# Input projection of a hybrid block in five passes instead of three, with TensorE's order tied to the recurrences

## The chip, the cores and the metric

The kernel runs on one NeuronCore of one Trainium2 chip. The metric is device time in microseconds (us). Three runs of the kernel before took 3179.27, 3181.92 and 3189.05 us; the median, 3181.92, is its time. Engines: PE (TensorE: matrix products; PEld are its weight loads), DVE (VectorE), ACT (ScalarE), POOL (GpSimd), SP (SyncE, which issues nearly all DMAs). Each takes its instructions strictly in the order in which they stand in the program.

## What is computed

One layer over 2048 tokens and 16 learned ones in front, all in float32. An input projection feeds three head groups: RG-LRU, forgetting attention and RWKV-7. Cut to what matters here:

```python
p = rms_norm(h, norm_mix_pre) @ w_in          # 1024 -> 512 (a) + 1544 (b) + 1024 (c) columns
oa = rg_lru_group(xa, ya, ...)                # from a: a scan over the tokens
ob = forgetting_attention_group(q, k, v, f)   # from b: softmax with the cumulative log of forget gates f
oc = rwkv7_group(pc, ...)                     # from c: S = S*w - (S kk)(kk a) + v k, out = S r, token by token
h = h + rms_norm(concat(oa, ob, oc) @ w_out, norm_mix_post)
f = causal_dwconv(rms_norm(h, norm_ffn_pre) @ ffn_up)
h = h + rms_norm((gelu(gate) * val) @ ffn_down, norm_ffn_post)
```

## The kernel before

Products that need float32 are split into rounded halves and done as three products (`mm3`, L150 to L152). Stages follow each other: input projection, attention, output projection (W_out), feed-forward up and down.

**Input projection.** The tokens are cut into three parts (784, 768 and 512), each of two blocks. For a part, `w_in_norm` loads its tiles of 128 tokens (7, 6 and 4), normalises and transposes them (tile `pst`, L121) and splits them into `xh` and `xl`, of which there is one set: a part's operands can be written only when the part before has been read. `w_in_part` then works through the weight columns in units of 128: first the forget gate (`psf`, L248), then twelve units for the recurrences (eight c, four a), then twelve for the attention (four each of k, v, q). A unit loads 512 KB of weights, splits them (ACT L144, DVE L145), makes 24 products for each of the two blocks (tile `psp`), evacuates them and stores them to DRAM: c and a to `scr_p`, the attention's to others. v is transposed first (`psv`). `core.evac` (L55, L57) takes ACT and DVE by turns.

**Recurrences.** They read `scr_p` in nine blocks of 256 tokens (the last has 64). `lru_block` is the RG-LRU. `Rwkv.block` prepares a block of RWKV: products for decay and rate (L869, L875), the norm of the keys (gat, L883), a reciprocal root on DVE (L73 to L77), its spreading (L902), the bonus (L922), then `chunks`: score matrices (L946), transposes (L975), a triangular solve on POOL and DVE (L989, L990) by way of DRAM, and, after the solve of the next block, the block's ending (L1013 to L1168: inverses, states, output, group norm). These products have the tiles `eps` (one PSUM bank) and `rps` (two banks). Both are written as generators; a `yield` ends a piece, some 13 to a block.

**What sets the order.** `Beside` holds the pieces. After part 0's gate and twelve units (`READY = 13`) they are added; from then on each unit is followed by `PACE = 1.5` pieces. After each third unit one step of `up_sums` (L1440 to L1449) loads 1 MB of feed-forward weights, forms four sums on POOL and stores them. What is left of the pieces is written out behind the last unit, the attention behind that. A scheduler then places the instructions of each engine by when it expects them ready, and the written order decides where several are; so an engine's order need not be the written one. `tc.issue_after(x)` tells it to place what is inside behind instruction x; it adds no wait between engines.

Of the kernel before, what the change touches and what calls it, by code (L numbers as in the profile page):

```python
# [12 lines left out]
AF = mybir.ActivationFunctionType  # L13
ALU = mybir.AluOpType
# [4 lines left out]
P = 128  # L19
# [166 lines left out]
def w_in_step(core, pools, psum, weights, block, kind, c0, scr):  # L186

    nc = core.nc
    wh, wl = weights
    st = pools["st"]  # L190
    t0, n, tl, hi, lo = block
    ps = psum.tile([P, 512], F32, tag="mm", name=core.n("psp"))
    for k in range(KD):
        mm3(nc, ps[:, :n], wh[:, k], wl[:, k], hi[:, k], lo[:, k], k == 0, k == KD - 1)
    if kind in ("q", "k"):
        sc = 0.125 if kind == "q" else 1.0
        r0 = c0 - (512 if kind == "q" else 1024)
        oh = st.tile([P, 400], F32R, tag="sth", name=core.n("sth"))
        ol = st.tile([P, 400], F32R, tag="stl", name=core.n("stl"), bufs=1)
        nc.scalar.activation(oh[:, :n], ps[:, :n], AF.Copy, scale=sc)  # L200
        nc.vector.scalar_tensor_tensor(ol[:, :n], ps[:, :n], sc, oh[:, :n], op0=ALU.mult, op1=ALU.subtract)
        nc.sync.dma_start(scr[kind + "h"][r0 : r0 + P, t0 : t0 + n], oh[:, :n].bitcast(F32))
        nc.sync.dma_start(scr[kind + "l"][r0 : r0 + P, t0 : t0 + n], ol[:, :n].bitcast(F32))
        return
    o = st.tile([P, 400], F32, tag="sth", name=core.n("stp"))
    core.evac(o[:, :n], ps[:, :n])
    if kind != "v":
        r0 = c0 if kind == "a" else c0 - 2056 + A_ROWS
        nc.sync.dma_start(scr["p"][r0 : r0 + P, PAD + t0 : PAD + t0 + n], o[:, :n])
        return  # L210

    def turn():

        r0 = c0 - 1536
        pt = psum.tile([P, 4, P], F32, tag="mm", name=core.n("psv"))
        for i, (s, rows) in enumerate(tl):
            nc.tensor.transpose(pt[:rows, i], o[:, s - t0 : s - t0 + rows], core.ident[:])
        ot = st.tile([P, 4, P], F32, tag="stv", name=core.n("stv"), bufs=1)
        i0 = 0
        if tl[0][1] < P:  # L220
            s, rows = tl[0]
            core.evac(ot[:rows, 0], pt[:rows, 0])
            nc.sync.dma_start(scr["v"][s : s + rows, r0 : r0 + P], ot[:rows, 0])
            i0 = 1
        m = len(tl)
        core.evac(ot[:, i0:m], pt[:, i0:m])
        s = tl[i0][0]
        nc.sync.dma_start(
            scr["v"][s : s + P * (m - i0), r0 : r0 + P].rearrange("(j p) c -> p j c", p=P), ot[:, i0:m]
        )  # L230

    return turn
# [22 lines left out]
    yield  # L255


def w_in_part(core, pools, psum, w_in, blocks, scr):
    yield from w_in_gate(core, pools, psum, w_in, blocks, scr)
    units = [("c", 2056 + P * i) for i in range(8)] + [("a", P * i) for i in range(4)]  # L260
    units += [(s, c + P * i) for s, c in (("k", 1024), ("v", 1536), ("q", 512)) for i in range(4)]
    waiting = [None]

    def step(*args):

        after = w_in_step(core, pools, psum, *args, scr)
        if waiting[0]:
            waiting[0]()
        waiting[0] = after

    for kind, c0 in units[:-2]:
        w = w_in_weights(core, pools, w_in, c0)
        for block in blocks:
            step(w, block, kind, c0)
        yield

    last = [(w_in_weights(core, pools, w_in, c0), kind, c0) for kind, c0 in units[-2:]]
    for block in blocks:
        for w, kind, c0 in last:
            step(w, block, kind, c0)  # L280
        yield
# [109 lines left out]
class Attn:  # L391
# [248 lines left out]
    AHEAD = 2  # L640
# [66 lines left out]
CH = 64  # L707
# [91 lines left out]
class Rwkv:  # L799
# [127 lines left out]
    def chunks(self, b, nch, sg, rav, bk, wc, bon):  # L927
# [38 lines left out]
        for q in range(parts):  # L966
            nc.sync.dma_start(ia[q * nblk : (q + 1) * nblk, :], da[:ni].rearrange("i q s t -> (i q) (s t)"))
        bkv = bk[:].rearrange("p c a t -> p c (a t)")
        tt(bkv, bkv, wc[:].to_broadcast([P, m2, 2 * CH]), op=ALU.mult)
        for c in range(0, m2, 4):  # L970
            m = min(4, m2 - c)
            for src, dst in ((bk, sc), (rav[:, :, 1:3], w3)):
# [85 lines left out]
        for i0 in range(0, ni, 4):  # L1058
# [5 lines left out]
            nc.scalar.activation(w3[0:64, i0 : i0 + m, 0:64], ps[0:64, :m, 64:128], AF.Copy)  # L1064
        yield
        gt, rp = self.t([P, m2, CH], "gt"), rav[:, :, 0]
        tt(
            gt[:], k["id2"][:].rearrange("p (o t) -> p o t", o=1).to_broadcast([P, m2, CH]),
            wc[:].to_broadcast([P, m2, CH]), op=ALU.mult,
        )  # L1070
# [150 lines left out]
def lru_block(core, R, scr, k, b):  # L1221
# [50 lines left out]

    ya = R.raw(256, c0, c0 + n)
    nc.scalar.activation(y, ya, AF.Square)
    nc.vector.tensor_scalar(y, y, 0.044715, 1.0, op0=ALU.mult, op1=ALU.add)
    tt(y, y, ya, op=ALU.mult)
    nc.scalar.activation(y, y, AF.Tanh, scale=0.7978845608028654)
    stt(y, y, 1.0, ya, op0=ALU.add, op1=ALU.mult)
    stt(u, u, 0.5, y, op0=ALU.mult, op1=ALU.mult)
# [410 lines left out]

READY = 13
PACE = 1.5

WIDE = (0, 5)

# [5 lines left out]
class Beside:  # L1703
# [14 lines left out]
                self.gens.pop(0)  # L1718
        return False

    def advance(self):
        self.due += self.pace if self.gens else 0.0
        while self.due >= 1.0:
            self.due -= 1.0
            if not self.step():
                break
# [31 lines left out]
def hybrid_block_kernel(ctx: ExitStack, tc: tile.TileContext, args, out):  # L1758
# [8 lines left out]
    def run(gen):  # L1767
        for _ in gen:
            pass
# [14 lines left out]
    with ExitStack() as p1:  # L1784
        core.const = pool(p1, "const1", 1)
        dp = pool(p1, "dp", 2, space=DRAM)
        rec = ExitStack()
        ps_rw = pool(rec, "ps_rw", 2, space=PSUM, **right)
        ps_ae = pool(rec, "ps_ae", 1, space=PSUM, **right)
        gp = pool(rec, "gp", 1, **right)  # L1790
        rp = pool(rec, "rp", 1, **right)
        with ExitStack() as p1a:
            ps_mm = pool(p1a, "ps_mm", 5, space=PSUM)
            g_pre = spread(pool(p1a, "gpre", 1), a["norm_mix_pre"], "g_pre")
            pools = {"xn": pool(p1a, "xn", 1), "nt": pool(p1a, "nt", 4), "w": pool(p1a, "w", 2), "st": pool(p1a, "st", 2)}
            sums = up_sums(core, pool(p1a, "us", 1), a["ffn_up"], scr)
            following = w_in_norm(core, pools, ps_mm, x, meta, g_pre, 0)
            for part in range(3):
                blocks = following
                if part == 0:  # L1800
                    zeros = pools["st"].tile([P, PAD], F32, tag="sth", name="zeros")
                    nc.vector.memset(zeros[:], 0.0)
                    for r in range(0, A_ROWS + C_ROWS, P):
                        nc.gpsimd.dma_start(scr["p"][r : r + P, 0:PAD], zeros[:])
                units = w_in_part(core, pools, ps_mm, a["w_in"], blocks, scr)
                for _ in range(READY if part == 0 else 0):
                    next(units)
                if part == 0:
                    attn_consts(core)
                    rk = rwkv_consts(  # L1810
                        core, gp, ps_ae,
                        {
                            s[5:]: (v.rearrange("h d -> (h d)") if s == "rwkv_r_k" else v)
                            for s, v in a.items() if s.startswith("rwkv_")
                        },
                    )
                    lk = lru_consts(
                        core, gp, ps_ae,
                        {
                            "conv_w": a["lru_conv_w"], "conv_b": a["lru_conv_b"], "ga_w": a["lru_gate_a_w"],  # L1820
                            "ga_b": a["lru_gate_a_b"], "gx_w": a["lru_gate_x_w"], "gx_b": a["lru_gate_x_b"],
                            "lam": a["lru_lambda"],
                        },
                    )
                    columns(core, gp, ps_ae, [a["ffn_conv"].rearrange("i (r p) -> (i r) p", p=P)], "", cw)
                    R = Rwkv(core, rp, dp, ps_rw, ps_ae, scr, rk)
                    beside = Beside(PACE)
                for i, _ in enumerate(units, READY + 1 if part == 0 else 1):
                    if i == READY + 1:
                        beside.add(recurrences(core, R, lk, a["fox_f_bias"], scr, blocks, part))  # L1830
                    beside.advance()
                    if i % 3 == 0:
                        next(sums, None)
                run(sums) if part == 2 else None
                if part < 2:
                    following = w_in_norm(core, pools, ps_mm, x, meta, g_pre, part + 1)
        beside.finish()
        for _ in R.ending:
            pass
        rec.close()  # L1840
        p2 = ExitStack()
        ps_wo = [pool(p2, "ps_wo", 2, space=PSUM, **right)]
        with ExitStack() as p1b:
            more = pool(p1b, "ps_more", 1, space=PSUM, **right, **early)
            at = Attn(core, pool(p1b, "ap", 2, **early), pool(p1b, "ps_at", 1, space=PSUM), more, scr)
            at.run()
# [142 lines left out]
```

## Time and profile before

| | us |
|---|---|
| median of three runs | 3181.92 |
| profiled execution | 3194.05 |
| its span, first to last instruction | 3192.3 |
| first and last column product (`psp`) of the input projection starts | 43.5 and 900.9 |
| last RWKV product of the tile `rps` (L1129) starts | 1202.4 |
| attention: first and last product of the tile `sc` starts | 911.4 and 1678.3 |
| PE, DVE, ACT, POOL busy in the span | 2984.6, 2191.1, 1446.3, 1252.4 |

The profile comes from one execution. Busy times of PE are modelled, as products are pipelined: a product's record lasts longer than the distance to the next one's start. In a row of a window stand: the stretch, its length, then busy us and records of PE, PEld, DVE, ACT and POOL, the granted PE clock as a share of full speed, the share of the DMA engines, and GB/s; rows of one tile have the same columns, without engines that don't touch it. In a group's row stand line, engine, operation, output and inputs, shapes, count | busy us, mean ns of one | idle time ahead of them and what ended it. In a timeline's row: start, us, engine, line, operation; in brackets the idle time ahead.

### The profile page before, as it was taken

The page shows a single profiled execution, that of the slowest core. Times are in us where ns is not written, and L with a number is a line of the kernel's source. Part 1 is how long each engine was busy: PE and PEld are TensorE (multiplying, and loading weights), DVE is VectorE, ACT ScalarE, POOL GpSimd, SP SyncE. Part 2 cuts the span into 40 slices and gives each one's busy share as a digit, 9 for nine tenths or more (in the row PEclk, how much of TensorE's full clock was granted, in tenths as well). Part 3 has the DMA queues.
Part 4 walks back from the last instruction along what each step waited for, and adds up shares of the span by engine and source line. Part 5 has one row for each costly group of instructions (what it writes and reads, how often), then busy time and mean ns, then how long its engine had stood idle before and what let it go on. Part 6 is the DMA issues. An engine that isn't in the chain of part 4 may idle for free. (4 is left out here: it accounts for less than half of the span.)

```text
span 3192.3 us, 52868 instructions
## 1 busy us (share of the span) xinstructions
PE 2984.6 (93%) x18509; PEld 2484.5 (78%) x18509; DVE 2191.1 (69%) x4623; ACT 1446.3 (45%) x2723; POOL 1252.4 (39%) x1419
## 2 busy tenths in 40 slices
PE   6988899999989898999998899999999999998998
PEld 6977788988965554555456799999999998786776
DVE  6147664776677767666748687787778777648777
ACT  3134333444534434444543466666666665324322
POOL 3334321001123345444752135434533345657555
PEclk8989899999978878999999999999999999999999
DMA  6777743443352336435416355555555554323454
GB/s 195 228 227 235 218 131 99 121 120 108 106 129 61 70 76 155 107 96 126 94 46 221 126 187 168 166 176 177 166 160 164 166 168 141 122 97 112 145 158 139
DMA packets 483051, 455.27 MB, mean 143 GB/s; under 512 B 82560, under 2 KB 407498, under 8 KB 478416
## 3 DMA queue, kind: packets, MB, share of 16 engines
q1 hardware_dynamic: 481888, 451.42, 48.6%
q8 instruction: 146, 2.39, 0.3%
q14 instruction: 121, 0.99, 0.1%
q0 software_dynamic: 384, 0.39, 0.0%
q10 hardware_dynamic: 512, 0.07, 0.0%
HBM read 336.31 MB, written 115.39 MB: 141 GB/s over the span
## 5 line engine op out<-in xcount | busy, mean ns | idle before, releaser
L150 PE MATMUL psu<-xo,uw 128*128 128x344 f32 x1848 | 588.8, 323 | 10.3 <-DVE wx L1345 4.8
L151 PE MATMUL psu<-xo,uw 128*128 128x344 f32 x1848 | 593.8, 322 | 1.0 <-DVE xo L1417 1.0
L152 PE MATMUL psu<-xo,uw 128*128 128x344 f32 x1848 | 582.6, 320 | 0.0
L152 PE MATMUL psp<-xh,wl 128*128 128x384 f32 (+2 forms) x1152 | 382.0, 332 | 3.6 <-DVE wl L145 3.6
L150 PE MATMUL psp<-xh,wh 128*128 128x384 f32 (+2 forms) x1152 | 385.1, 334 | 0.2 <-DVE xl L128 0.2
L151 PE MATMUL psp<-xl,wh 128*128 128x384 f32 (+2 forms) x1152 | 382.1, 332 | 0.0
L150 PEld LDWEIGHTS psu<-xo,uw 128*128 128x128 f32 x1848 | 347.6, 189 | 11.8 <-DVE wx L1345 5.2
L151 PEld LDWEIGHTS psu<-xo,uw 128*128 128x128 f32 x1848 | 348.9, 189 | 1.3 <-DVE xo L1417 1.3
L152 PEld LDWEIGHTS psu<-xo,uw 128*128 128x128 f32 x1848 | 347.3, 189 | 0.0
L1416 ACT ACTIVATE uw<-uq 128x512 fp32r<-128x512 f32 x462 | 287.2, 627 | 110.6 <-PE psu L152 56.2
L557 ACT ACTIVATE p<-sc,bias 128x512 f32<-128x512 f32 (+2 forms) x360 | 203.8, 585 | 261.5 <-PE sc L555 227.0
L1417 DVE TENSOR_TENSOR uw<-uq,uw 128x512 fp32r<-128x512 f32 x330 | 280.9, 856 | 60.2 <-ACT uw L1416 54.9
L587 POOL TENSOR_TENSOR acc<-acc,p 128x512 f32<-128x512 f32 (+3 forms) x208 | 224.8, 1081 | 175.1 <-ACT p L557 118.0
L1501 DVE SCALAR_TENSOR_TENSOR uy<-psu,ffn_cols,uy 128x342 f32<-128x342 f32 (+1 forms) x396 | 224.6, 569 | 94.6 <-ACT uy L1499 93.6
L1417 POOL TENSOR_TENSOR uw<-uq,uw 128x512 fp32r<-128x512 f32 x132 | 182.1, 1380 | 270.8 <-ACT uw L1416 191.2
L1507 POOL TENSOR_TENSOR uy<-uy,uy 128x342 f32<-128x342 f32 (+1 forms) x132 | 139.4, 1056 | 317.2 <-DVE uy L1501 137.0
L491 DVE TENSOR_REDUCE mc<-mx 128x1 f32<-128x400 f32 (+5 forms) x320 | 173.0, 556 | 100.9 <-PE mx L488 97.4
L152 PEld LDWEIGHTS psp<-xh,wl 128*128 128x128 f32 x1152 | 222.6, 193 | 11.9 <-issue 5.5
L150 PEld LDWEIGHTS psp<-xh,wh 128*128 128x128 f32 x1152 | 222.3, 193 | 7.4 <-issue 4.6
L151 PEld LDWEIGHTS psp<-xl,wh 128*128 128x128 f32 x1152 | 222.2, 193 | 7.3 <-issue 5.4
L566 PE MATMUL po<-p,v 128*64 128x512 f32 (+3 forms) x720 | 183.3, 548 | 5.2 <-POOL p L559 2.3
L1416 ACT ACTIVATE fo<-u 128x896 fp32r<-128x896 f32 x88 | 80.9, 922 | 225.5 <-POOL u L1623 123.1
(425 smaller groups left out, 6479.3 us busy)
## 6 DMA issues: line engine op xcount, KB each, us to landing
uq<-scr_us SPq DMA_DIRECT2D x264, 256.0 KB
uq<-in_ffn_up_dram SPq DMA_DIRECT2D x198, 256.0 KB
raw<-in_w_in_dram SPq DMA_DIRECT2D x72, 512.0 KB
us<-in_ffn_up_dram SPq DMA_DIRECT2D x44, 512.0 KB
scr_us<-us SPq DMA_DIRECT2D x22, 1024.0 KB
u<-scr_ff SPq DMA_DIRECT2D x88, 256.0 KB
scr_ff<-uy SPq DMA_DIRECT2D x110, 171.0 KB
q<-scr_qh SPq DMA_DIRECT2D x96, 128.0 KB
```

The costliest lines, as they stand in the source:

```text
L150: nc.tensor.matmul(out, ah, bh, start=first, stop=False, skip_group_check=more)
L151: nc.tensor.matmul(out, ah, bl, start=False, stop=False, skip_group_check=more)
L152: nc.tensor.matmul(out, al, bh, start=False, stop=last, skip_group_check=more)
L491: self.reduced = nc.vector.tensor_reduce(mc[:rows, i, ci : ci + 1], ps[:rows, :full], axis=AX.X, op=ALU.max)
L557: last = nc.scalar.activation(p[:rows, :w], ps[:rows, :w], AF.Exp, bias=bias[:rows, j : j + 1])
L566: mm = nc.tensor.matmul(po[64 * i : 64 * i + 64, c0:n], v1[:rows, j], p[:rows, : n - c0], start=jj == 0, stop=jj + i + 2 >= len(kt), tile_ ...
L587: eng.tensor_tensor(a, ps_[0][:rows, c0:n] if jj == 0 else a, p[:rows, : n - c0], op=ALU.add)
L1416: core.nc.scalar.activation(hi, src, AF.Copy)
L1417: (eng or core.nc.vector).tensor_tensor(lo, src, hi, op=ALU.subtract)
L1501: stt(y[:, :n], src[:, i : n + i], cw[:, 44 * i + cc : 44 * i + cc + 1], y[:, :n], op0=ALU.mult, op1=ALU.add)
L1507: core.pooled = nc.gpsimd.tensor_tensor(v[:, :n], g[:, :n], v[:, :n], op=ALU.mult)
```

## The change

- The projection runs in five passes. Passes 0, 1 and 2 make the gate and the recurrences' columns of the three parts; pass 2 goes on with the attention's columns of its part, pass 3 makes those of part 1, pass 4 those of part 0. Parts 1 and 0 are normalised and transposed again for that: 30 tiles instead of 17.
- Recurrences of a part join when its columns are done. `PACE` is 2.1 for 768 tokens, less or more by a unit's share of them.
- From the start of the recurrences on, each unit is placed behind the last PE instruction written out when the unit two back and its pieces were done (`held`, `AHEAD = 1`): its loads, splits, products and stores.
- The weight sums begin with pass 1, one step to every second unit.
- Evacuations of c, a and v go to ACT alone. Four elementwise operations go from DVE to POOL: bk x wc (ahead of the transposes L975), gt, and two of the RG-LRU's gelu.

```diff
-    core.evac(o[:, :n], ps[:, :n])
+    nc.scalar.activation(o[:, :n], ps[:, :n], AF.Copy)
...
+RECURRENT = [("c", 2056 + P * i) for i in range(8)] + [("a", P * i) for i in range(4)]
+ATTENDED = [(s, c + P * i) for s, c in (("k", 1024), ("v", 1536), ("q", 512)) for i in range(4)]
+def w_in_part(core, pools, psum, w_in, blocks, scr, recurrent, attended):
+    units = []
+    if recurrent:
+        yield from w_in_gate(core, pools, psum, w_in, blocks, scr)
+        units += RECURRENT
+    if attended:
+        units += ATTENDED
...
-        tt(bkv, bkv, wc[:].to_broadcast([P, m2, 2 * CH]), op=ALU.mult)
+        nc.gpsimd.tensor_tensor(bkv, bkv, wc[:].to_broadcast([P, m2, 2 * CH]), op=ALU.mult)
...
-    nc.vector.tensor_scalar(y, y, 0.044715, 1.0, op0=ALU.mult, op1=ALU.add)
-    tt(y, y, ya, op=ALU.mult)
+    nc.gpsimd.tensor_scalar(y, y, 0.044715, 1.0, op0=ALU.mult, op1=ALU.add)
+    nc.gpsimd.tensor_tensor(y, y, ya, op=ALU.mult)
...
-READY = 13
-PACE = 1.5
+READY = 1 + len(RECURRENT)
+PACE = 2.1
+AHEAD = 1
+PASSES = (0, True, False), (1, True, False), (2, True, True), (1, False, True), (0, False, True)
...
-    def advance(self):
-        self.due += self.pace if self.gens else 0.0
+    def advance(self, share):
+        self.due += self.pace * share if self.gens else 0.0
...
+            def product():
+                return next(i for i in reversed(nc.cur_bb.bb.instructions) if i.engine == mybir.EngineType.PE)
+            for at_, (part, recurrent, attended) in enumerate(PASSES):
...
+                share = sum(n for _, n, *_ in blocks) / 768
+                i = 1 if at_ == 1 else 0
+                while True:
+                    with tc.issue_after(held.pop(0)) if len(held) > AHEAD else nullcontext():
+                        if next(units, 0) == 0:
+                            break
+                    i += 1
+                    if due:
+                        beside.add(recurrences(core, R, lk, a["fox_f_bias"], scr, due[1], due[0]))
+                        due = None
+                    if recurrent and i == READY:
+                        due = part, blocks
+                    if beside.gens:
+                        beside.advance(share)
+                        held.append(product())
+                    if at_ and i % 2 == 0:
+                        next(sums, None)
-                run(sums) if part == 2 else None
...
+            run(sums)
```

How it moves TensorE's order is seen best where a block of RWKV is prepared. In the program of before, around the products L883 (gat, squared keys) and L902 (spreading of the root) of block 0, PE has

```order
L883 MATMUL eps_213_1705<-rwsq_212_1702,gat_1182 4x256 x2
L217 MATMUL psv_282_2117<-ident_58,stp_277_2081 128x128 x2
L150 MATMUL psp_288_2154<-xh_1_123,wh_285_2148 128x400
L151 MATMUL psp_288_2154<-xl_2_124,wh_285_2148 128x400
...
L151 MATMUL psp_326_2336<-xl_2_124,wh_323_2330 128x400
L152 MATMUL psp_326_2336<-xh_1_123,wl_324_2331 128x400
L902 MATMUL eps_217_1730<-rwix_215_1709,spr_1184 128x256
```

with 70 rows from the one to the other. In the changed program (lines there are eight higher: L877 and L883 for L869 and L875, L891 for L883, L910 for L902, L930 for L922, L954 for L946) PE has for block 1

```order
L152 MATMUL psp_334_2391<-xh_134_1140,wl_330_2358 128x384
L877 MATMUL eps_310_2282<-rwwa_303_2260,wa_up_1401 128x256
L883 MATMUL eps_311_2286<-rwwa_303_2260,wa_up_1401 128x256
L883 MATMUL eps_312_2289<-rwwa_303_2260,wa_up_1401 128x256
L891 MATMUL eps_314_2295<-rwsq_313_2292,gat_1410 4x256 x2
L910 MATMUL eps_318_2320<-rwix_316_2299,spr_1412 128x256
L910 MATMUL eps_319_2323<-rwix_316_2299,spr_1412 128x256
L930 MATMUL eps_327_2350<-rwsq_313_2292,bones_1406 128x256
L954 MATMUL rps_338_2421<-rwrav_322_2334,rwbk_324_2341 128x128
```

so the columns between the steps are gone there. It differs from block to block: no column stands between L891 and L910 in blocks 0, 1, 2 and 6, 20 to 50 rows' worth in 3 and 4, and 65 or more in 5, 7 and 8; none between the second L910 and the first L954 in six of the nine.

The second place is the end of the projection. In the program of before PE has, from the last column product on (`mx`, `sc`: attention),

```order
L152 MATMUL psp_9533<-xh_6191,wl_9314 128x256
L902 MATMUL eps_8820<-rwix_8727,spr 128x256
L902 MATMUL eps_8823<-rwix_8727,spr 128x256
L922 MATMUL eps_8850<-rwsq_8720,bones 128x256
L554 MATMUL sc_10992<-q_1493_10930,k_1483_10903 16x16
L488 MATMUL mx_10937<-k_1484_10904,q_1486_10908 16x16
```

which is in the preparation of block 6, and in the changed program

```order
L152 MATMUL psp_10729<-xh_8759,wl_10576 128x384
L983 MATMUL rps_10769<-ident,rwbk_10672 128x128 x2
L983 MATMUL rps_10773<-ident,rwrav_10665 128x128 x2
L1021 MATMUL rps_10821<-rwxu_10812,rwsc_9677 32x32 x32
L1021 MATMUL rps_10855<-rwxu_10812 32x32 x16
L1021 MATMUL rps_10873<-rwxu_10812 32x32 x32
```

which is in block 8, the short one, and the ending of block 7. Of 2313 recurrence products (rows with a count taken in full) 860 stood behind the last column product before, and 294 do now; the attention's products ahead of the first one of W_out are 648 and 637.

More of the change, by code (lines that the diff above doesn't have):

```diff
@@ L221, in turn @@
             s, rows = tl[0]
-            core.evac(ot[:rows, 0], pt[:rows, 0])
+            nc.scalar.activation(ot[:rows, 0], pt[:rows, 0], AF.Copy)
             nc.sync.dma_start(scr["v"][s : s + rows, r0 : r0 + P], ot[:rows, 0])
@@ L225, in turn @@
         m = len(tl)
-        core.evac(ot[:, i0:m], pt[:, i0:m])
+        nc.scalar.activation(ot[:, i0:m], pt[:, i0:m], AF.Copy)
         s = tl[i0][0]
@@ L255, in w_in_gate @@
     yield
[L258 to L261, printed above, removed]
+RECURRENT = [("c", 2056 + P * i) for i in range(8)] + [("a", P * i) for i in range(4)]
[7 more added lines that the diff above has]
+        units += ATTENDED
     waiting = [None]
@@ L1066, in chunks @@
         gt, rp = self.t([P, m2, CH], "gt"), rav[:, :, 0]
-        tt(
+        nc.gpsimd.tensor_tensor(
             gt[:], k["id2"][:].rearrange("p (o t) -> p o t", o=1).to_broadcast([P, m2, CH]),
@@ L1797, in hybrid_block_kernel @@
             following = w_in_norm(core, pools, ps_mm, x, meta, g_pre, 0)
-            for part in range(3):
+            due, held = None, []
+            beside = Beside(PACE)
+            def product():
+                return next(i for i in reversed(nc.cur_bb.bb.instructions) if i.engine == mybir.EngineType.PE)
+            for at_, (part, recurrent, attended) in enumerate(PASSES):
                 blocks = following
-                if part == 0:
+                if at_ == 0:
                     zeros = pools["st"].tile([P, PAD], F32, tag="sth", name="zeros")
@@ L1804, in hybrid_block_kernel @@
                         nc.gpsimd.dma_start(scr["p"][r : r + P, 0:PAD], zeros[:])
-                units = w_in_part(core, pools, ps_mm, a["w_in"], blocks, scr)
-                for _ in range(READY if part == 0 else 0):
+                units = w_in_part(core, pools, ps_mm, a["w_in"], blocks, scr, recurrent, attended)
+                if at_ == 1:
                     next(units)
-                if part == 0:
                     attn_consts(core)
@@ L1826, in hybrid_block_kernel @@
                     R = Rwkv(core, rp, dp, ps_rw, ps_ae, scr, rk)
[L1827 to L1832, printed above, removed]
+                share = sum(n for _, n, *_ in blocks) / 768
[14 more added lines that the diff above has]
+                    if at_ and i % 2 == 0:
                         next(sums, None)
-                run(sums) if part == 2 else None
-                if part < 2:
-                    following = w_in_norm(core, pools, ps_mm, x, meta, g_pre, part + 1)
+                if at_ + 1 < len(PASSES):
+                    following = w_in_norm(core, pools, ps_mm, x, meta, g_pre, PASSES[at_ + 1][0])
+            run(sums)
         beside.finish()
```

## The prediction

> **What bounds the kernel now.** I read the page first, then busy time by stage, then single tiles and lines.
>
> ```profile
> span 3192.3 us, 52868 instructions
> PEclk8989899999978878999999999999999999999999
> ```
>
> The granted clock of TensorE (PE) falls in the first five slices and in slices 11 to 15, the stretches to look into. The span stands 1.75 us under its execution's 3194.05 us, which is 12.1 above the median of the runs, 3181.92. The stages, with busy time by engine, clock and DMA:
>
> ```profile
> 0.00:165.00 165.00, 135.40 (x725) 131.60 (x726) 65.83 (x189) 44.67 (x70) 60.99 (x60) 0.93 0.70 208
> 165.00:300.00 135.00, 118.43 (x625) 109.28 (x624) 82.46 (x160) 52.37 (x98) 44.90 (x36) 0.92 0.76 236
> 300.00:345.00 45.00, 28.02 (x128) 22.09 (x127) 38.10 (x82) 24.49 (x48) 19.35 (x20) 0.73 0.79 225
> 400.00:640.00 240.00, 234.52 (x2060) 212.06 (x2058) 148.44 (x344) 92.39 (x160) 33.16 (x49) 0.98 0.40 117
> 640.00:680.00 40.00, 39.31 (x378) 36.08 (x379) 25.47 (x49) 19.33 (x38) 3.03 (x4) 0.93 0.40 108
> 680.00:895.00 215.00, 214.13 (x2242) 193.30 (x2241) 146.88 (x341) 101.42 (x188) 18.49 (x39) 0.99 0.39 109
> 895.00:1210.00 315.00, 281.24 (x2292) 178.06 (x2290) 229.14 (x780) 121.52 (x285) 117.49 (x207) 0.78 0.37 86
> 1210.00:1690.00 480.00, 451.00 (x1848) 242.68 (x1847) 322.38 (x811) 212.70 (x386) 236.72 (x277) 0.98 0.43 103
> ```
>
> From 400 to 895 PE has no time left. From 895 to 1210 it runs the rest of the recurrences with the first attention steps, at clock 0.78, with 34 us idle: the change aims at this stage. What follows leads up to W_out's first product, at 1287.6:
>
> ```profile
> L150 PE MATMUL pswo<-woh,mh x272: 387/389/792, 1287.6 to 1787.0; 128*128 128x512 f32 x128, 128*2 128x512 f32 x8
> ```
>
> From there the program is the same before and after, so I ask when this product starts. What of the stage was whose:
>
> ```profile
> 0.00:1690.00 1690.00, 250.38 (x4162) 209.45 (x4162) 106.98 (x233) 54.92 (x111) 0.93 0.48 131
> 895.00:1210.00 315.00, 111.05 (x1596) 92.43 (x1596) 41.58 (x96) 20.46 (x42) 0.78 0.37 86
> 895.00:1210.00 315.00, 21.92 (x64) 11.03 (x64) 6.67 (x18) 6.25 (x16) 0.78 0.37 86
> 895.00:1210.00 315.00, 6.13 (x52) 5.92 (x50) 2.15 (x3) 1.15 (x3) 0.78 0.37 86
> ```
>
> These are the tile rps over the recurrences' whole time and in the stage, then eps and psp in the stage. So of the 281 us 133 were recurrences, 6 the last columns and 142 attention, which then had another 78 us up to W_out (1210 to 1287.6).
>
> **The change, part by part.** *Pass 0* (gate and twelve units, as before). By 165 PE had 725 records; 664 are this pass and its transposes, the other 61 at 0.18 us take 11, so it ends at 154. Then the next tokens must be normalised. Before, that took from 304.67 to 334.08, 29 us, and I take as much: pass 1 starts at **183**.
>
> ```profile
> 304.67 1.91 PE L121 MATMUL pst<-ident,xt 128*128 128x128 f32 x16
> 334.08 0.67 PE L248 MATMUL psf<-xh,fw 128*128 128x384 f32 x1
> ```
>
> *Column products of passes 1 to 4.* Their price is the distance of starts:
>
> ```profile
> 400.52 0.34 PE L150 MATMUL psp<-xh,wh 128*128 128x384 f32 x1
> 400.70 0.34 PE L151 MATMUL psp<-xl,wh 128*128 128x384 f32 x1
> ...
> 699.94 0.28 PE L150 MATMUL psp<-xh,wh 128*128 128x256 f32 x1
> 700.06 0.28 PE L151 MATMUL psp<-xl,wh 128*128 128x256 f32 x1
> ```
>
> 0.175 us with 384 tokens, 0.119 with 256 (means of longer stretches), 0.182 with 400 by proportion. Passes 1 and 3: 12 units of 48, 101 us each; pass 2: 24 of 48 at 0.119, 137; pass 4: 12 of 24 and 24, 103. The gates add 9. Normalising is done for 30 tiles instead of 17; the 17 that come after pass 1 began cost
>
> ```profile
> L121 PE MATMUL pst<-ident,xt 128*128 128x128 f32 (+1 forms) x136 | 26.1, 359 | 29.1 <-DVE xt L108 24.3 <-DVE stl L201 4.0 <-DVE xl L128 0.7
> ```
>
> 26 us of PE. Sum **477**.
>
> *Recurrences beside them.* In the two saturated stages I take the columns off:
>
> ```profile
> 400.00:640.00 240.00, 174.55 (x874) 155.40 (x872) 15.46 (x28) 10.15 (x21) 0.98 0.40 117
> 680.00:895.00 215.00, 148.96 (x1067) 133.93 (x1066) 13.34 (x32) 9.78 (x26) 0.99 0.39 109
> ...
> 400.00:640.00 240.00, 54.79 (x1104) 46.61 (x1104) 25.43 (x55) 12.99 (x26) 0.98 0.40 117
> 680.00:895.00 215.00, 59.77 (x1084) 49.44 (x1084) 27.23 (x59) 13.10 (x26) 0.99 0.39 109
> ```
>
> (psp, then rps.) 240 - 874 x 0.175 = 87 and 215 - 1067 x 0.119 = 88, so 175 us for 2188 records: 0.080 each, with eps, the transposes of v and every small wait in it. In TensorE's order 860 rows of recurrences stood behind the last column product; now 294 do. The 860 were 1596 records, so 294 are some 546, and the other 3616 at 0.080 cost **289**. Columns and recurrences would then end at 183 + 477 + 289 = 949.
>
> *The waits that the order adds.* A unit's products now stand behind the recurrence product that was written out one unit earlier, so only one unit is free to run beside a chain. In the rows shown above, a block has no column product from the second L877 to L954; before, some 70 rows of columns stood between the gat product and the next alone. There PE now waits for the chain in full:
>
> ```profile
> L870 ACT ACTIVATE rwe<-eps,rwkv_om 128x256 f32<-128x256 f32 x16 | 7.5, 470 | 11.5 <-DVE rwk L1279 8.4 <-PE eps L869 3.0
> L75 DVE SCALAR_TENSOR_TENSOR rwitmp<-rwix 4x256 f32<-4x256 f32 x24 | 10.0, 415 | 0.1
> L76 DVE TENSOR_TENSOR rwitmp<-rwitmp,rwia 4x256 f32<-4x256 f32 x24 | 12.5, 521 | 0.2
> L77 DVE SCALAR_TENSOR_TENSOR rwix<-rwitmp,rwix 4x256 f32<-4x256 f32 x24 | 12.0, 500 | 0.3
> L903 DVE SCALAR_TENSOR_TENSOR rwk<-rwk,rwkv_cols,eps 128x256 f32<-128x256 f32 x16 | 7.7, 479 | 15.2 <-PE eps L902 15.1
> L905 DVE SCALAR_TENSOR_TENSOR rwe<-rwe,rwk 128x512 f32<-128x512 f32 x8 | 5.9, 742 | 0.0
> L912 DVE TENSOR_TENSOR rwrav<-rwk,rwe 128x512 f32<-128x512 f32 x8 | 5.5, 685 | 0.0
> ```
>
> First leg: four evacuations with their products, 3.8 us, in five blocks without columns between: 19. Second: three rounds of L75 to L77 and two small ones, about 4.7, with some 2.8 of other VectorE work queued among them, 7.5, in four blocks in full and two in part: 37. Third: two L903, L905 and two like L912, 3.8, in six blocks: 23. Together **80**. Bounds: 0, if unit and chain meet otherwise in time than in rows, and 150, if VectorE's queue, 65% busy beside the columns (148.44 of 240), stretches the chain twofold. Behind a waiting product stand all later columns, hence their evacuations and SP's stores.
>
> *The clock.* What a wait does to it:
>
> ```profile
> 395.30 1.22 PE L1251 MATMUL eps<-rwk,lru_gx_w 128*128 128x256 f32 x2 [4.86 <-DVE rwe L1249]
> 396.64 0.52 PE L152 MATMUL psp<-xh,wl 128*128 128x384 f32 x1
> 396.96 0.52 PE L150 MATMUL psp<-xh,wh 128*128 128x384 f32 x1
> ```
>
> After 4.86 us of waiting the distance is 0.32 us instead of 0.175 until 400.16, about 2 us lost. With some ten such waits I put **20** (0 to 40). [...]
>
> *Boundaries.* Two more are added, and recurrences run through three. Before, one cost 17 us of idle PE (300 to 345), the other nothing (640 to 680): **15** for all (0 to 34). *Weight sums* start later and more thinly, which spares pass 0 and the stretch from 165 to 300 some DMA pressure: **-10** (-22 to 0). *Offloads*: the copies leave VectorE (0.55 us) for ScalarE (0.49), which is 39% busy from 400 to 640: nothing, or 0.5 us a unit without that cover. bk x wc on GpSimd:
>
> ```profile
> L1446 POOL TENSOR_TENSOR us<-us 128x512 f32<-128x512 f32 x22 | 35.4, 1611 | 1.6
> POOL us L1445 <- DMA us<-in_ffn_up_dram: 209.3, 19, 17.5
> ```
>
> It takes some 3.2 us there (two 512-wide ones), hidden by 3 to 8 us of columns ahead of the transposes; the other offloads have no product waiting. Taken as 0; uncovered, 3.2 x 8 = 26 at most, and below nothing by what VectorE no longer does. Projection ends at 949 + 80 + 20 + 15 - 10 = **1054**.
>
> *Behind it.* 546 records at 0.083 (133 us over 1596) are 45, and the attention runs beside them with nothing else to fill its gaps. Its 142 at clock 0.78 become 126 at 0.88, midway to the 0.98 of the stage behind (113 at that clock; 176 if it keeps the clock and takes all of the 34 idle); 78 stay; 15 idle I take instead of 34. W_out starts at 1054 + 45 + 126 + 78 + 15 = 1318, **30 us later**: 3194 + 30 = 3224 profiled, 3212 on the median's scale.
>
> **The rivals.** *A, the waits are covered, faster.* For it: from 400 to 895 PE already hides the chain; one free unit is 8.4 us, more than any single leg. Against it: the rows of blocks 0, 1, 2 and 6. Without waits and clock loss, 100 less: about 3112. The point is 70: with waits and clock loss together under 70 us the change is no slower, with under 60 it is faster. *B, the chain is stretched,* because GpSimd works more: SP's and POOL's queues now mix weight sums into all recurrences, and a POOL sum waited 11 us for its DMA (209.3 over 19). Waits of 150: 70 more, 3282. [...] *C, no change:* waits and clock near 70, 3182. That the order is not what the text says is out: 294 rows for 860; but a kept order may still not shorten the recurrences, which is B.
>
> **How the numbers follow.** Within 0.3% (about what a measurement tells from no change, 9.5 us): 12%. A has 40%, since the waits' lower bound is as near as the upper one. The forecast's case has 34% and B 14%, slower together 48%. Bounds added all one way, without the forecast's own values, give some 120 us either side of 3212; cases A and B reach from 3112 to 3282, and the range, 3110 to 3280, leaves out about a tenth on each side.
>
> **What would show it.** Right: idle PE before L910 and L954, released by VectorE, some 80 us in all; PE under 95% busy and clock under 0.95 between 200 and 1050; the last psp near 1054; W_out's first product near 1318. Wrong: the last psp before 990, or the attention's first steps at clock 0.95 and above, each of which makes it faster.

## The result, and the profile after

The changed kernel took 3352.07 us (median of four runs, 3349.31 to 3355.47), the kernel before 3183.27 beside it: a ratio of 1.0535, 95% interval 1.0516 to 1.0553. The forecast, 3212, had the sign and not the size. The profiled execution of after took 3355.47 us. Its page begins, first the span, then the granted clock by slices:

```profile
span 3353.8 us, 53369 instructions
PEclk8977888979889878899999999999999999999999
```

Where before had nines in six slices from the sixth on, after has mostly eights and sevens up to slice 17. W_out's first product of after, from the view of the tile pswo:

```profile
L150 PE MATMUL pswo<-woh,mh x272: 387/389/793, 1448.4 to 1950.5; 128*128 128x512 f32 x128, 128*2 128x512 f32 x8
```

It starts 160.8 us later (1287.6 before), and the span is 161.5 longer: the whole loss stands ahead of W_out. The windows up to the last column product, from there to W_out, and both, of before and then of after (columns as before: stretch, length, busy us of PE, PEld, DVE, ACT, POOL, clock, DMA share, GB/s):

```profile
0.00:900.90 900.90, 825.30 (x6539) 756.86 (x6539) 540.43 (x1229) 353.54 (x633) 203.01 (x230) 0.95 0.55 161
900.90:1287.60 386.70, 337.43 (x2483) 201.43 (x2483) 285.68 (x912) 155.63 (x348) 155.79 (x255) 0.81 0.42 98
0.00:1287.60 1287.60, 1162.73 (x9020) 958.28 (x9021) 826.11 (x2140) 509.17 (x981) 358.80 (x485) 0.90 0.51 142
```

```profile
0.00:1145.00 1145.00, 961.51 (x7730) 857.28 (x7731) 650.09 (x1557) 453.35 (x855) 251.59 (x303) 0.87 0.46 135
1145.00:1448.40 303.40, 252.97 (x1380) 134.91 (x1380) 199.81 (x640) 107.55 (x237) 132.97 (x216) 0.79 0.48 113
0.00:1448.40 1448.40, 1214.48 (x9109) 992.19 (x9110) 849.90 (x2197) 560.90 (x1092) 384.55 (x519) 0.85 0.46 131
```

Of the 161 us, 109 are idle PE (233.9 against 124.9) and 52 more busy PE (1214.5 against 1162.7). The projection ends 244 us later; the stretch behind it is only 83 shorter, although two thirds of its recurrence products have left it. What PE waits for in passes 1 to 4 of after (the view of waits; engine, tile, line, who released it: us in all, times, longest):

```profile
PE eps L910 <- DVE rwix L77: 36.6, 5, 9.2
PE eps L877 <- ACT rwe L878: 18.0, 7, 5.9
PE rps L954 <- DVE rwbk L921: 9.1, 6, 3.9
PE rps L1105 <- DVE rwst L1109: 8.3, 7, 2.7
PE rps L983 <- POOL rwbk L977: 7.6, 3, 6.2
PE eps L883 <- ACT rwe L878: 7.4, 5, 2.9
PE eps L883 <- ACT rwe L884: 4.6, 4, 2.6
PE eps L910 <- DVE rwk L911: 4.4, 5, 2.1
PE eps L891 <- ACT rwsq L888: 4.0, 2, 3.6
PE eps L891 <- ACT rwe L884: 3.5, 5, 1.6
PE eps L930 <- DVE rwk L911: 3.4, 6, 0.6
```

Not one of these is a column product that waits for its operands (in the whole view those come to 1.7 us): all are steps of the chain, which PE stands in front of. One of them in the timeline, PE first, then DVE:

```profile
670.03 0.28 PE L152 MATMUL psp<-xh,wl 128*128 128x256 f32 x1
670.15 0.38 PE L217 MATMUL psv<-ident,stp 128*128 128x128 f32 x2
676.62 1.22 PE L910 MATMUL eps<-rwix,spr 4*128 4x256 f32 x2 [6.09 <-DVE rwix L77]
```

```profile
672.45 0.41 DVE L77 SCALAR_TENSOR_TENSOR rwix<-rwitmp,rwix 4x256 f32<-4x256 f32 x1
672.79 1.21 DVE L145 TENSOR_TENSOR wl<-raw,wh 128x1024 fp32r<-128x1024 f32 x1
673.92 0.41 DVE L75 SCALAR_TENSOR_TENSOR rwitmp<-rwix 4x256 f32<-4x256 f32 x1
...
676.15 0.41 DVE L77 SCALAR_TENSOR_TENSOR rwix<-rwitmp,rwix 4x256 f32<-4x256 f32 x1
```

The one unit that was free has run out at 670, and the reciprocal root is still at its first round, whose L77 starts at 672.45. DVE splits a later unit's weights between two rounds (L145, 1.21 us): those products are not needed yet, since they stand behind L910. The next unit's weights had been split by 664.14 (the L145 ahead of this one), and its first product starts at 684.82, behind L910, L930 and L954.

### The profile page after: what moved, and what is told of

Same layout as the page of the kernel before. It is cut to its first block, busy times and chain, and to the rows that moved or that the text cites. A ratio compares the mean times of both kernels' runs of the same rounds, so it can differ in the third digit from the quotient of the medians.

```text
span 3353.8 us, 53369 instructions
## 1 busy us (share of the span) xinstructions
PE 3042.2 (91%) x18613; PEld 2520.0 (75%) x18613; DVE 2217.2 (66%) x4681; ACT 1500.8 (45%) x2837; POOL 1282.5 (38%) x1455
```

## The experiments

Ratios are to the kernel before, run beside each on the same chip, with 95% intervals; medians of before differ from call to call (3183.27 to 3200.14 us), so ratios are compared. The theories: **H**, the kept order makes PE wait; **O**, the offloads stretch the chain; **P**, the five passes cost it.

**No hold** (after):

```diff
-AHEAD = 1
+AHEAD = 1000
```

> The changed kernel without the hold: AHEAD = 1000, so that no unit is placed behind a recurrence product; passes, pace and offloads stay. Up to W_out's first product the changed kernel has 109 us more idle PE than the kernel before and 52 us more busy PE. Theory H (the kept order makes PE wait for the chain): most of the 109 and some of the cold clock go, 3240 to 3280 us, and PE's wait before L910 falls from 36.6 to under 10 us. Theory O (the offloads stretch the chain): no change, 3335 to 3365. Theory P (five passes: second normalisation, more boundaries, attention without recurrences beside it): at most 40 us of gain, 3310 to 3350.

3225.91 us, 1.010 (1.0079 to 1.0121). In its windows and waits:

```profile
0.00:963.80 963.80, 869.47 (x6912) 789.36 (x6913) 592.20 (x1373) 423.48 (x786) 249.92 (x276) 0.93 0.54 159
963.80:1318.30 354.50, 317.34 (x2201) 187.25 (x2200) 249.52 (x822) 133.59 (x305) 146.49 (x243) 0.80 0.44 102
```

```profile
PE eps L877 <- ACT rwe L878: 3.6, 2, 2.2
PE eps L910 <- DVE rwix L77: 1.2, 2, 0.9
```

W_out at 1318.3: 130 us earlier than in after, 102 of them idle PE (131.5 against 233.9), 28 busy. L910 waits 1.2 us instead of 36.6. H, even under its lower end; four fifths of the loss is the hold.

**The hold alone** (before, with `AHEAD = 1` and PACE still 1.5):

```diff
-                for i, _ in enumerate(units, READY + 1 if part == 0 else 1):
+                while True:
+                    with tc.issue_after(held.pop(0)) if len(held) > AHEAD else nullcontext():
+                        if next(units, 0) == 0:
+                            break
...
+                    if beside.gens:
+                        held.append(product())
```

> The kernel before with the hold alone (AHEAD = 1) at its own PACE of 1.5, three passes, no offloads. Theory H: 60 to 110 us slower than before, 3240 to 3290, with columns gone between the steps of a block's preparation and waits at L877, L902 and L946's counterparts. Theories O and P: within 20 us of before, 3165 to 3205.

3322.01 us, 1.0399 (1.0368 to 1.0429): H, above the range. PE's largest wait in sum, up to 1288 us, is the counterpart of after's:

```profile
PE eps L902 <- DVE rwix L77: 30.9, 4, 12.5
```

So the hold costs some 4% in both programs, whatever the passes.

**The offloads alone** (before) **and undone** (after): the evacuations and the four operations as the change's diff has them, and the same backwards.

```diff
-        tt(bkv, bkv, wc[:].to_broadcast([P, m2, 2 * CH]), op=ALU.mult)
+        nc.gpsimd.tensor_tensor(bkv, bkv, wc[:].to_broadcast([P, m2, 2 * CH]), op=ALU.mult)
...
```

> The kernel before with the offloads alone: evacuations of c, a and v on ACT, four elementwise operations on POOL. Theory O: over 40 us slower, 3225 or more, with PE waiting for POOL before L975. Theories H and P: 3165 to 3200, the offloads being worth no more than 15 us either way where columns cover them.

> The changed kernel with the offloads undone (alternating evacuations, the four operations on DVE again); five passes and the hold stay. Theory O: 3300 or less. Theory H: between 3335 and 3370, since what is taken from DVE returns to the queue in which the chain's own steps stand, and what POOL cost (waits of 7.6 us before L983) goes. Theory P: the same as H.

1.0004 (0.9984 to 1.0023) alone; undone in the changed kernel 1.0555 (1.0523 to 1.0586) against 1.0535. O falls: they are worth nothing that shows, in either program.

**Three passes, no hold** (before with the offloads, PACE 2.1, a weight sum to every second unit):

```diff
-PACE = 1.5
+PACE = 2.1
...
-                    if i % 3 == 0:
+                    if i % 2 == 0:
```

> The changed kernel without the hold and with three passes again: the kernel before with the offloads, PACE 2.1 and one weight sum to every second unit. Theory P1 (the five passes cost what is left of the loss without the hold, by second normalisation and the waits at two more boundaries): 3180 to 3205, some 30 us under the run without the hold. Theory P2 (pace and sums cost it): 3215 or more, as without the hold.

3189.11 us, 0.9977 (0.9959 to 0.9995). Against 1.010 with five passes and no hold, the passes cost 1.2%, some 39 us, with the other order of the columns that goes with them. That is P's share.

**Two more free units** (after):

```diff
-AHEAD = 1
+AHEAD = 3
```

> The changed kernel with AHEAD = 3, so that each unit stands behind the recurrence product written out four units earlier instead of two. Without the hold 3226, with it 3352. Theory H1 (what is missing is column products to fill the steps of the chain: two more free units, some 17 us, are more than any single wait, the longest being 9 us): most of the 126 us comes back, 3235 to 3275. Theory H2 (columns and chain are coupled as such: each unit waits for the chain however far ahead it may run, and the chain sets the rate): 3310 or more, and the period of a block stays at 100 to 130 us.

3329.28 us, 1.0421 (1.0403 to 1.0439): H1's range missed by far, H2's met. In its waits (window 180 to 1120) the longest one for L77 grew, from 9.2 to 14.2 us:

```profile
PE eps L910 <- DVE rwix L77: 52.4, 5, 14.2
```

The two more units do not lie in that step. Between a block's last gat product and its first L910 no column product stands in blocks 0, 1, 2 and 6, in after's trace as in this one; there PE waits 6.5 to 9.2 us in after and 8.1 to 14.2 here. (Without the hold 47 to 107 stand there in blocks 0 to 6, and no wait is over 0.9 us.) Where 29 or more stand, it does not wait, but for one block here (61 products, 6.2 us). So H1 was wrong about where AHEAD = 3 puts columns, not shown wrong about what is missing.

The distance of blocks, from the first to the last gat product, in before, after and this run (36 records, nine blocks, so a block is an eighth of the stretch):

```profile
L883 PE MATMUL eps<-rwsq,gat x36: 219/379/631, 243.1 to 1064.5; 128*4 128x256 f32 x32, 128*4 128x64 f32 x4
```

```profile
L891 PE MATMUL eps<-rwsq,gat x36: 219/590/634, 239.7 to 1114.3; 128*4 128x256 f32 x32, 128*4 128x64 f32 x4
```

```profile
L891 PE MATMUL eps<-rwsq,gat x36: 219/379/631, 249.2 to 1100.1; 128*4 128x256 f32 x32, 128*4 128x64 f32 x4
```

102.7, 109.3 and 106.4 us a block. These are means: single distances go from 78 to 151 us in before and from 71 to 142 in after. Nor is it the same rate in every run, as the next expectation has it: the hold alone gives 115.0. H2 took it for the chain's own rate, which the next runs tried.

**A slower pace**, with AHEAD 1 and 3 (after):

```diff
-PACE = 2.1
+PACE = 1.2
```

> The changed kernel with PACE = 1.2 and the hold as it is (AHEAD = 1). The squared keys' products (gat) of two blocks after another stand 102 to 109 us apart in every run so far, with and without the hold, while a unit (8.4 us) and 2.1 pieces ask for a block each 77 us (13 pieces: 6.2 units and 25 us of recurrence products). At 1.2 they ask for one each 116 us. Theory H2 (the hold ties the columns to a chain that cannot go faster): the chain now keeps up, the last column product starts at 950 to 1020 and the time is 3235 to 3290. Theory H1 (each step of the chain without columns beside it costs its wait): only two or three blocks' waits fewer, 3305 to 3335.

> The changed kernel with PACE = 1.2 and AHEAD = 3. Theory H2: with the rate right, the two more free units cover what is left of single waits: 3225 to 3260, as without the hold, and at least 15 us under PACE 1.2 with AHEAD 1. Theory H1: as AHEAD 3 at PACE 2.1 showed, 20 us under the run with AHEAD 1, and over 3285.

3346.5 us, 1.0455 (1.0438 to 1.0473), and 3281.54, 1.026 (1.0233 to 1.0288). Of the first:

```profile
0.00:947.60 947.60, 813.61 (x6085) 752.24 (x6086) 500.59 (x1138) 356.55 (x655) 212.12 (x232) 0.90 0.53 156
947.60:1441.30 493.70, 413.85 (x3030) 249.07 (x3030) 340.84 (x1047) 199.52 (x433) 177.93 (x288) 0.74 0.34 79
```

The columns did end near where H2 said, 947.6, but the time did not follow: now the chain is late, at 124.8 us a block, and 494 us lie between the columns and W_out instead of 303. H2 in its simple form falls. H1's range for the first is missed by the median and met by the ratio (1.0455 of the 3183 beside which after was run is 3328); the second lies between both theories' ranges. With both edits 2.7% come back in ratios.

**Few columns** (after): the attention's columns (k, v, q) keep one of eight slices of their products, so most of what they compute is left out.

```diff
+    ks = range(KD) if kind in ("a", "c") else range(1)
-    for k in range(KD):
...
+    for k in ks:
...
```

> The changed kernel with an eighth of the products of the attention's columns (k, v, q): 24 instead of 192 for each unit and block pair of 384 tokens and alike, so that 7/8 of 377 us, about 330 us of TensorE's work, are left out, 239 of them in passes 2 to 4. What it computes for the attention is left out with them. Pass 0 and 1 keep their work. Theory H2 (from pass 2 on the chain's own rate sets the end): blocks stay 95 to 110 us apart and W_out's first product moves by less than 60 us, 3290 or more. Theory H1 (columns and waits add up): the 239 us come off nearly in full, W_out's first product before 1270, under 3170.

3243.81 us, 1.0137 (1.0117 to 1.0157), W_out at 1336.4: of 239 us of columns taken out of passes 2 to 4, 112 come off, between both theories. (A unit keeps 6 of its 48 products for each pair of blocks, and the attention's columns are made in passes 2 to 4 alone, so the 239 us are all that is left out; the expectation's 377 and 330 are wrong.) Its gat products (one line lower) and its projection:

```profile
L892 PE MATMUL eps<-rwsq,gat x36: 268/630/635, 239.9 to 996.7; 128*4 128x256 f32 x32, 128*4 128x64 f32 x4
```

```profile
0.00:1026.40 1026.40, 797.35 (x6201) 678.63 (x6201) 642.17 (x1535) 448.05 (x849) 256.64 (x301) 0.75 0.51 149
```

94.6 us a block on the mean, and 87 over the last five, which have 24 to 120 column products beside them, at a clock of 0.75 up to the last column product. So the chain with little beside it, at this clock, is not far under the 103 that it takes beside full columns.

**Eight units ahead**, at both paces (after):

```diff
-AHEAD = 1
+AHEAD = 8
```

> The changed kernel with AHEAD = 8 at its PACE of 2.1. Theory M (a block takes the longer of two: about 103 us that the chain needs whatever runs beside it, or the work that PACE puts beside it plus the waits that are not covered; at PACE 2.1 the work is 77 us, so the chain is the longer, and each unit of AHEAD is worth its own 8.4 us once): seven units more than the changed kernel, 59 us off 3352, 3275 to 3310. Theory H1 (missing columns beside single steps, covered by a few units): as without the hold, 3225 to 3255. Theory H2 (the chain alone, whatever AHEAD): over 3320.

> The changed kernel with PACE = 1.2 and AHEAD = 8. AHEAD 1 gave 3346 at this pace, AHEAD 3 3281. Theory M: here the work (118 us a block) is the longer and only uncovered waits add to it (27 and 17 us a block with AHEAD 1 and 3), which eight units cover: 3225 to 3255, as without the hold. Rival (the pieces that PACE 1.2 leaves behind the last column cost it, 1196 products against 715 without the hold): 3265 or more.

3262.57 us, 1.0204 (1.0175 to 1.0232), and 3269.07, 1.023 (1.0204 to 1.0256). At PACE 2.1 W_out moved 91 us, 34 of which AHEAD = 3 had given; M said 59 (seven units of 8.4), the others over 100 or under 30. In ratios the gain is 3.3%, 105 us of 3183, the size that H1 gave. So a unit of slack gives more than its own work, and M's sum does not hold. The step ahead of L910 now has columns in it, 33 to 73 products in blocks 0 to 7, and one of its waits is left (7.4 us; the others are 0.3 and less). At PACE 1.2 the rival is right:

```profile
0.00:873.70 873.70, 795.31 (x5996) 737.89 (x5997) 487.34 (x1113) 354.26 (x652) 207.24 (x230) 0.94 0.57 169
873.70:1354.20 480.50, 407.93 (x3121) 250.17 (x3120) 349.65 (x1079) 201.05 (x434) 179.84 (x289) 0.77 0.35 81
```

Its columns end first of all, 873.7, and W_out still comes at 1354.2. The runs side by side:

| PACE, AHEAD | last column product | from there to W_out | ratio |
|---|---|---|---|
| 2.1, 1 (after) | 1145.0 | 303 | 1.0535 |
| 2.1, 3 | 1121.6 | 293 | 1.0421 |
| 2.1, 8 | 1031.1 | 326 | 1.0204 |
| 2.1, none | 963.8 | 354 | 1.010 |
| 1.2, 1 | 947.6 | 494 | 1.0455 |
| 1.2, 3 | 897.7 | 469 | 1.026 |
| 1.2, 8 | 873.7 | 480 | 1.023 |

**Weight sums later** (before; each step's loads stand behind the last DMA written for SP ahead of them), and the same with the offloads, PACE 2.1 and a sum to every second unit:

```diff
-                        next(sums, None)
+                        with tc.issue_after(stored()):
+                            next(sums, None)
```

> The kernel before with the loads of each weight sum placed behind the last DMA that stands ahead of them in writing on SP's queue, so that sums go on until the end of the projection instead of being done by 431 us. The prediction gave later sums -10 us (-22 to 0) by less DMA pressure from 165 to 345 us. If that holds: 3160 to 3185, with less idle PE up to 345 us. Rival: a later sum's store and loads block w's loads in SP's queue: 3200 or more, with column products waiting for DVE and DMA.

> The kernel before with the offloads, PACE 2.1 (no hold, three passes) and the later weight sums, one to every second unit: the two edits that came out at 0.998 and 0.999 of before together. If what they spare adds up, 3170 to 3185; if the attention's first half, which starts earlier, ends where it did because the last recurrences do, 3185 to 3195.

0.999 (0.9973 to 1.0007), and together 0.9954 (0.9939 to 0.997): 3184.0 us against 3200.14, 16 us faster than before and the largest gain among the runs. Alone, the later sums cannot be told from no change; their median lies between the two ranges. First before, then the later sums alone:

```profile
0.00:345.00 345.00, 281.85 (x1474) 262.96 (x1475) 186.38 (x429) 121.52 (x216) 125.23 (x115) 0.90 0.73 221
```

```profile
0.00:345.00 345.00, 306.93 (x1689) 290.64 (x1690) 190.78 (x466) 132.40 (x230) 48.17 (x67) 0.97 0.55 159
871.70:1281.60 409.90, 357.48 (x2481) 217.96 (x2482) 291.26 (x901) 157.16 (x349) 176.52 (x272) 0.76 0.47 113
```

Up to 345 PE has 25 us less idle, and the columns end at 871.7 instead of 900.9. But the stretch behind them is 410 us instead of 387, and W_out comes only 6 us earlier (one execution of each).

## Why the prediction was right in sign and wrong in size

The sign was little better than even: the prediction gave slower 48% and faster 40%. The forecast put the projection's end at 1054 and W_out at 1318; they came at 1145 and 1448. Passes 1 to 4 of after:

```profile
183.00:1145.00 962.00, 825.31 (x7010) 726.56 (x7011) 558.04 (x1298) 386.82 (x741) 189.43 (x236) 0.87 0.41 119
```

- *Pass 0 and the normalising behind it*, 183: right. The first product of pass 1 stands at 184.9.
- *Busy PE*, forecast 477 + 289 + 20 for the clock = 786: 825, so 39 short, and the mis-sized term is the **clock**. A mean of 0.87 over 962 us means half speed in a quarter of it (0.13 x 2 x 962 = 250 us; the trace's clock records, each 1.0 or 0.5, give 258 at 0.5); the forecast priced ten waits of 2 us. Reckoned from the trace, the products that ran at half clock in this stretch took some 82 us longer than products of the same line and shape at full clock in it (distance of starts, less waits), 51 of them on products of the recurrences; the rest came to 743, which is 23 under the price of 766. The chain's own small products slow down with the clock: the median gat product took 590 ns against 379 before (rows above), and within after 631 in the 24 records at half clock against 379 in the other 12.
- *Waits*, forecast 80: the three legs named took 37.5 (L877, L883, L891), 41.0 (L910) and 12.5 (L954, L930), together 91, against 19, 37 and 23. The second leg was right in place and size, the first took twice its price and the third half of it.
- *Idle PE in all*, 80 + 15 for boundaries = 95: 962 - 825 = 137, 42 short, 11 of them in the legs. The rest is at steps for which the forecast had no term: L983 and L1105 above, the transposes ahead of the solve and the states, took 16 us, and further ones lie below in the same view with up to 3.2 us each. What the 15 stood for, waits of normalising and of columns, came to about 4.
- *Weight sums*, -10: not moved at all. Their stores in after, against a projection that goes on to 1145:

```profile
L1457 SPq DMA_DIRECT2D scr_us<-us x22: 319/339/419, 38.1 to 424.8; - x22
```

  The written order alone did not decide their place. Moved in earnest they spare 25 us of idle PE, more than the bound of 22, of which 6 reach W_out (one execution of each).
- *Offloads*, 0: right in both programs.
- *Behind the projection*, 264: 303. Busy 253 as forecast (45 + 126 + 78 = 249), but idle 50 where 15 was taken: the attention's own waits stay when the recurrences leave (38 of the 50 stand ahead of its products; before, 49 of 387 were idle).

These add up: 39 + 42 + 10 = 91 to the projection's end, 39 behind it, 130 in all.

The rivals. A, waits covered, is out. B's price (waits of 150) came nearer the time than the forecast did, but not by its mechanism: GpSimd's part was tried alone and is nothing, and the weight sums, done by 425, never mixed into all recurrences.

The steps that failed are three terms of the sum: the clock (20, measured 82), the idle PE of the projection (80 + 15, measured 137) and the idle PE behind it (15, measured 50); the -10 of the weight sums did not come. They came out small because they were counted per block, as if columns and chain were two stacks of work with a few gaps. The experiments show two streams in one engine, PE, that takes them in order (the runs of one output tile on PE follow one another in both traces as in the programs, 1444 in before and 1344 in after), and that the hold ties to each other: it takes the column products out of steps of the chain, and PE stands there. That alone costs 4.0% in the program of before, and taking it away gives back 4.3 of after's 5.4%; what is left is about the price of the passes. With AHEAD 1, at PACE 2.1 the columns are late (1145), at 1.2 the chain is (494 us behind the columns), and only slack between them gives time back. The hold itself binds PE's products alone: a program in which it encloses only the column products has the order of the changed program on all five engines. The front of this document, which counts loads, splits and stores among what is placed, says too much there; L145 ahead of L75 in the timeline agrees with that.

What stays open is the law of it: how much of a unit's slack comes back (34 us for the first two units, 57 for the next five, 39 for all others, by W_out's start), and how much of that is the clock. No run held the clock and changed the waits.

## What to carry to other kernels

Be slow to tie one stream of work to another in an engine that takes both in order. With one free unit the kernel was 4.0 to 5.4% slower than before at every pace tried (1.2, 2.1, and 1.5 in three passes), and without the hold 1.0%. So the right pace is no remedy; free units are, once columns stand in the steps where the chain is waited for. Read off, too, the rate at which the other stream has gone: the row of L883 gives 103 us a block on the mean, while the new pace asks for one each 77. Eight blocks from 240 on, and 31 us from the last gat product to the last column product (known from after alone), end at 1092 at that rate, later than the 1054 of the sum. And a PE that is freed early is worth only what the stage behind can take: 29 us at the end of the columns were 6 at W_out.

## What the hardware showed that was not expected

The clock falls after shorter waits than the 4.86 us from which the prediction priced it. In after:

```profile
867.85 0.28 PE L1137 MATMUL rps<-rwst,rwrav 64*64 64x64 f32 x2
870.39 0.70 PE L1255 MATMUL eps<-rwk,lru_ga_w 128*128 128x256 f32 x2 [2.27 <-ACT rwsq L1260]
...
875.69 0.52 PE L151 MATMUL psp<-xl,wh 128*128 128x384 f32 x1
876.01 0.52 PE L152 MATMUL psp<-xh,wl 128*128 128x384 f32 x1
...
877.92 0.34 PE L152 MATMUL psp<-xh,wl 128*128 128x384 f32 x1
878.09 0.34 PE L150 MATMUL psp<-xh,wh 128*128 128x384 f32 x1
```

After a wait of 2.27 us, and small products of the chain behind it, the distance of the column products is 0.32 us at 876 and 0.17 again only at 878. Of the 21 stretches at half clock that the trace's clock records begin between 183 and 1145, 17 have no wait over 2.9 us in the 12 us ahead of them. One of these, which begins at 717.47, has no wait of PE at all in the 9 us ahead of it, only small products among the columns, whose distance goes from 0.12 to 0.21 us:

```profile
714.09 2.21 PE L1021 MATMUL rps<-rwxu 32*32 32x32 f32 x96
...
716.45 0.29 PE L151 MATMUL psp<-xl,wh 128*128 128x256 f32 x1
716.57 0.28 PE L152 MATMUL psp<-xh,wl 128*128 128x256 f32 x1
...
716.90 1.54 PE L1021 MATMUL rps<-rwxu,rwsc 32*32 32x32 f32 x32
...
718.75 0.41 PE L152 MATMUL psp<-xh,wl 128*128 128x256 f32 x1
718.96 0.41 PE L150 MATMUL psp<-xh,wh 128*128 128x256 f32 x1
```

So it is not a wait in those 9 us that sets the clock here; what does is not shown.
